# mLSTM state update: a zero-padded 128-column stationary for the 64-row part of each state product

## The chip, the cores and the metric

The kernel runs on one core of one Trainium2 chip. The metric is the device time of one execution in microseconds (us). Engines: PE is TensorE (PEld its weight loads), DVE VectorE, ACT ScalarE, POOL GpSimd, SP the engine that issues the transfers.

## What is computed

The reference is an encoder trunk of two layers on 1024 tokens of width 1024. Each layer normalises its input, projects it once, runs three groups of heads on the projection (mLSTM, HGRN2 and differential attention), gates their outputs and projects them back. The change lies in the mLSTM group: 4 heads of dimension 192, each run forwards and backwards over the sequence. The part of it that matters is the state of a chunk step:

```python
# mlstm_chunkwise, step(carry, inp): ws is exp(dec_s - m_new)
num = einsum("bhts,bhsd->bhtd", w, vb) + g_inter * einsum("bhtd,bhde->bhte", qb, C)
C_new = a * C + einsum("bhs,bhsd,bhse->bhde", ws, kb, vb)   # 192 x 192
n_new = a * n + einsum("bhs,bhsd->bhd", ws, kb)
```

## The kernel before, in words

The program is written in plain order, layer by layer; a scheduler of the tile framework then sets the order of each engine's instructions from its own estimate of their times, so work of different groups is interleaved. Everything is float32; the large projections split each operand into two float32r parts and run three products (L295 for outputs by channel, L308 for outputs by token).

The mLSTM recurrence (L573 to L657) loops over 4 heads (`hd`), over 8 chunks of 128 tokens (`i`) and over two directions (`d`). For each head it loads `xac` (two channel tiles, L581), `xct` (tokens by channels, L583), `vt` (values and a column of ones, 193 columns, L586) and the rows for `W` (L605), makes `q` (L592) and the masked weights `W` (L601 to L611). Then, for each of 16 steps:

- the output product `num` in one bank of PSUM: L627 (`W` by `vt`) into columns 0 to 192, L631 and L632 (`q` by the state `C`, in two tiles of 128 rows) into columns 256 to 448; ACT and DVE combine them and add the result to `hsum` (L633 to L656);
- for the first 7 steps of each direction the state product: GpSimd writes `ks`, the 128 x 192 keys scaled by the weights of their tokens (L639); PE multiplies them with `vt` in two parts, since 192 rows don't fit into one product: 128 key columns (L642) into `C[:, 0]` and 64 key columns (L643) into half of `C[:, 1]`; DVE adds both to the decayed state (L645, L646).

So there are 2 x 4 x 2 x 7 = 112 state products of two matmuls each. Which half of `C[:, 1]` is used depends on the head (`r0` is 0 for even heads, 64 for odd ones); the other half is zeroed once (L618). `ks` has two buffers for both directions together.

PE's order puts these steps between the matmuls of the HGRN2 heads: `hiz`, `hq`, `hff`, `hfb` (projections, 128 stationary columns), the transposes and products L790 to L836, and products with narrow stationaries: L712 and L736 (64 columns; the tiles `lv` hold levels of the HGRN2 scores), L753 and L755 (64 or 32 columns). For a projection block, SP loads four quarters `wraw` (L135), ACT rounds them to `whi` (L136) and GpSimd makes the rest `wlo` (L137); the blocks are numbered (`wlo10` is the `hiz` block of HGRN2 head 2, `wlo13` that of head 3, both in layer 0). SP issues all transfers, one after another, so a transfer that waits for its buffer holds up those behind it.

Of the kernel before, what the change touches and what calls it, by code (L numbers as in the profile page):

```python
# [9 lines left out]
F32 = mybir.dt.float32  # L10
# [4 lines left out]
ALU = mybir.AluOpType  # L15
AX = mybir.AxisListType

P = 128
# [7 lines left out]
MD = 192  # L26
# [64 lines left out]
def trunk(ctx, tc, x_in, positions, w_in, w_out, pvec, rvec, out, dbg=None):  # L91
    nc = tc.nc
# [254 lines left out]
    for l in range(DEPTH):  # L347
# [6 lines left out]
        mu_d = dr.tile([8, S], F32, name=f"mu_{l}")  # L354
        mpl_d = dr.tile([16, 8], F32, name=f"mpl_{l}")

        # ------------------------------------------------------------ input norm
        h = []
        if l:
            npool = ExitStack()  # L360
# [1 line left out]
        for half in range(2):  # L362
# [21 lines left out]
            for k in range(8):  # L384
                ps = ps_mx(f"hT{l}{half}{k}")
                for t4 in range(4):
# [3 lines left out]
                                               op0=ALU.mult, op1=ALU.subtract)  # L390
# [1 line left out]
        npool.close()  # L392
        hpool = ExitStack()
        gp = hpool.enter_context(tc.tile_pool(name=f"hg{l}", bufs=1))
        # ------------------------------------------------------------ mLSTM: conv, q/k/v, gates
        mpool = ExitStack()
        m1 = mpool.enter_context(tc.tile_pool(name=f"mg{l}", bufs=1))
        G = []
# [2 lines left out]
        with tc.tile_pool(name=f"ma{l}", bufs=2) as ma:  # L401
# [38 lines left out]
            for i in range(3):  # L440
                parts = load_win(l, ("xm", i)) if l or i else xm0
                for jj in range(2):
# [9 lines left out]
                    for k in (0, 1, 3, 4):  # L452
                        d = k - 2
# [114 lines left out]
                nc.scalar.activation(t, t, AF.Exp)  # L568
            nc.scalar.activation(flr, flr, AF.Exp, scale=-1.0)

        # ------------------------------------------------------------ mLSTM: chunk recurrence
        with tc.tile_pool(name=f"mc{l}", bufs=1) as mp:
            for hd in range(MH):  # L573
                pr_, hh_ = divmod(hd, 2)
                jA, jC = 3 * pr_ + 2 * hh_, 3 * pr_ + 1
                cA, cC = (slice(0, P), slice(P, MD)) if hh_ == 0 else (slice(64, MD), slice(0, 64))
                r0 = 64 * hh_
                ch = slice(hd * MD, (hd + 1) * MD)
                xac = mp.tile([P, 2, S], F32, tag="m8", name=f"xac{l}{hd}", bufs=2)
                for i, j in enumerate((jA, jC)):  # L580
                    nc.sync.dma_start(xac[:, i], xc_d[j])  # L581
                xct = mp.tile([P, NT, MD], F32, tag="xct", name=f"xcth{l}{hd}")
                nc.sync.dma_start(xct, xct_d.rearrange("(t p) c -> p t c", p=P)[:, :, ch])  # L583
                vt = mp.tile([P, NT, MD + 1], F32, tag="vt", name=f"vth{l}{hd}")
                nc.gpsimd.memset(vt[:, :, MD:], 1.0)
                nc.sync.dma_start(vt[:, :, :MD], v_d.rearrange("(t p) c -> p t c", p=P)[:, :, ch])  # L586
                q = mp.tile([P, 2, S], F32, tag="m8", name=f"q{l}{hd}", bufs=2)
                for i, g in enumerate((G[jA], G[jC][:, hh_])):
                    for half in range(2):
                        sl = slice(half * 512, (half + 1) * 512)  # L590
                        ps = ps_mx(f"q{l}{hd}{i}{half}")
                        nc.tensor.matmul(ps, g, xac[:, i, sl], start=True, stop=True)  # L592
                        nc.scalar.activation(q[:, i, sl], ps, AF.Copy)
                W = {}
                for half in range(2):
                    ps = ps_mx(f"qk{l}{hd}{half}")
                    for c4 in range(4):
                        c = half * 4 + c4
                        sl = slice(c * P, (c + 1) * P)
                        for i in range(2):  # L600
                            nc.tensor.matmul(ps[:, c4 * P:(c4 + 1) * P], xac[:, i, sl], q[:, i, sl], start=(i == 0), stop=(i == 1))  # L601
                    for d in range(2):
                        w = mp.tile([P, 4, P], F32, name=f"W{l}{hd}{half}{d}", tag="W", bufs=4)
                        wf = w.rearrange("p c t -> p (c t)")
                        nc.sync.dma_start(wf, mu_d[d * 4 + hd, half * 512:(half + 1) * 512].partition_broadcast(P))  # L605
                        for c4 in range(4):
                            nc.scalar.activation(w[:, c4], w[:, c4], AF.Exp, scale=-1.0, bias=a_tok[:, d, half * 4 + c4, hd:hd + 1])
                        sg = 1 if d == 0 else -1
                        nc.gpsimd.affine_select(w, w, pattern=[[0, 4], [sg, P]], compare_op=ALU.is_ge, fill=0.0,
                                                base=0, channel_multiplier=-sg)  # L610
                        nc.vector.tensor_tensor(wf, wf, ps, op=ALU.mult)  # L611
                        for c4 in range(4):
                            W[(d, half * 4 + c4)] = w[:, c4]
                hsum = mp.tile([P, NT, MD], F32, tag="m8", name=f"hsum{l}{hd}", bufs=2)
                Cs = []
                for d in range(2):
                    C = mp.tile([P, 2, MD + 1], F32, name=f"C{l}{hd}{d}", tag="C", bufs=2)
                    nc.gpsimd.memset(C, 0.0)  # L618
                    Cs.append(C)
                seen = set()  # L620
                for i in range(NT):
                    for d in range(2):
                        c = i if d == 0 else NT - 1 - i
                        C = Cs[d]
                        sl = slice(c * P, (c + 1) * P)
                        pn = ps_mx(f"num{l}{hd}{d}{c}")
                        nc.tensor.matmul(pn[:, :MD + 1], W[(d, c)], vt[:, c], start=True, stop=True)  # L627
                        n = mp.tile([P, MD + 1], F32, name=f"n{l}{hd}{d}{c}", tag="n", bufs=2)
                        if i > 0:
                            pi = pn[:, 256:256 + MD + 1]  # L630
                            nc.tensor.matmul(pi, q[:, 0, sl], C[:, 0], start=True, stop=False)  # L631
                            nc.tensor.matmul(pi, q[:, 1, sl], C[:, 1], start=False, stop=True)  # L632
                            nc.scalar.activation(n, pi, AF.Copy, scale=ginter[:, d, c, hd:hd + 1])  # L633
                            nc.vector.tensor_tensor(n, pn[:, :MD + 1], n, op=ALU.add)
                        else:
                            nc.scalar.activation(n, pn[:, :MD + 1], AF.Copy)
                        if i < NT - 1:
                            ks = mp.tile([P, MD], F32, name=f"ks{l}{hd}{d}{c}", tag="ks", bufs=2)
                            nc.gpsimd.tensor_scalar(ks, xct[:, c], wsv[:, d, c, hd:hd + 1], None, op0=ALU.mult)  # L639
                            pc = ps_mx(f"st{l}{hd}{d}{c}")  # L640
                            pc2 = pc[r0:r0 + 64, 256:256 + MD + 1]
                            nc.tensor.matmul(pc[:, :MD + 1], ks[:, cA], vt[:, c], start=True, stop=True)  # L642
                            nc.tensor.matmul(pc2, ks[:, cC], vt[:, c], start=True, stop=True)  # L643
                            dc = dec[:, d, c, hd:hd + 1]
                            nc.vector.scalar_tensor_tensor(C[:, 0], C[:, 0], dc, pc[:, :MD + 1], op0=ALU.mult, op1=ALU.add)  # L645
                            nc.vector.scalar_tensor_tensor(C[r0:r0 + 64, 1], C[r0:r0 + 64, 1], dc[r0:r0 + 64], pc2,  # L646
                                                           op0=ALU.mult, op1=ALU.add)
                        den = mp.tile([P, 1], F32, name=f"den{l}{hd}{d}{c}", tag="den", bufs=4)
                        nc.vector.scalar_tensor_tensor(den, n[:, MD:], -1.0, n[:, MD:], op0=ALU.mult, op1=ALU.max)
                        nc.vector.tensor_tensor(den, den, flr[:, d, c, hd:hd + 1], op=ALU.max)  # L650
                        nc.vector.reciprocal(den, den)
                        if c not in seen:
                            seen.add(c)
                            nc.vector.tensor_scalar_mul(hsum[:, c], n[:, :MD], den)
                        else:
                            nc.vector.scalar_tensor_tensor(hsum[:, c], n[:, :MD], den, hsum[:, c], op0=ALU.mult, op1=ALU.add)  # L656
                nc.sync.dma_start(hs_d[hd], hsum)  # L657
        mpool.close()

        # ------------------------------------------------------------ HGRN2  # L660
        def slab(name, tag, bufs=None):
            return gp.tile([P, S], F32, tag=tag, name=f"{name}{l}", bufs=bufs or 1)

# [174 lines left out]
            nc.scalar.activation(yo, ps, AF.Copy, scale=hgs[:, l, hd:hd + 1])  # L838
            nc.sync.dma_start(yT[6 + hd], yo)

        # ------------------------------------------------------------ mLSTM: output gates
        md = hpool.enter_context(tc.tile_pool(name=f"md{l}", bufs=1))

        mo = {}
# [51 lines left out]
            {"i": hgrn_iz, "r": hgrn_rest, "o": mlstm_om, "z": mlstm_zm}[step[0]](int(step[1]))  # L896
        hpool.close()

        # ------------------------------------------------------------ attention
        with tc.tile_pool(name=f"at{l}", bufs=2) as ap, tc.tile_pool(name=f"aw{l}", bufs=1) as aw:  # L900
            def o_post(hd, gt, ss, r):
                rstd(ss, r, P)
# [125 lines left out]
                pend = (hd, gt, ss, r)  # L1028
            o_post(*pend)

        # ------------------------------------------------------------ output projection
        xs = []
        for half in range(2):
            xt = big_tile([P, 4, D], F32, f"xo{l}{half}")
# [122 lines left out]
```

## Time and profile before

| | |
|---|---|
| runs | 2908.21, 2910.12, 2915.83 us, median 2910.12 |
| profiled execution, span from first to last instruction | 2911.1 us (its time beyond the span isn't given) |
| granted TensorE clock, mean | 0.991 |
| PE / DVE / ACT / POOL busy | 97 / 63 / 37 / 22% |

The profile lists one execution. A group names the line, the engine, the operation and the tiles (out<-in), the shape and the number of instructions. A float32 matmul stands as two weight loads and two passes, so 112 matmuls give x224. A matmul counts as busy until a modelled end, and successive matmuls overlap; how long one really takes shows in the distance between two starts.

### The profile page before, as it was taken

The page shows a single profiled execution, that of the slowest core. Times are in us where ns is not written, and L with a number is a line of the kernel's source. Part 1 is how long each engine was busy: PE and PEld are TensorE (multiplying, and loading weights), DVE is VectorE, ACT ScalarE, POOL GpSimd, SP SyncE. Part 2 cuts the span into 40 slices and gives each one's busy share as a digit, 9 for nine tenths or more (in the row PEclk, how much of TensorE's full clock was granted, in tenths as well). Part 3 has the DMA queues.
Part 4 walks back from the last instruction along what each step waited for, and adds up shares of the span by engine and source line. Part 5 has one row for each costly group of instructions (what it writes and reads, how often), then busy time and mean ns, then how long its engine had stood idle before and what let it go on. Part 6 is the DMA issues. An engine that isn't in the chain of part 4 may idle for free. (4 is left out here: it accounts for less than half of the span.)

```text
span 2911.1 us, 49951 instructions
## 1 busy us (share of the span) xinstructions
PE 2821.4 (97%) x20004; PEld 2467.5 (85%) x20004; DVE 1847.9 (63%) x4054; ACT 1070.5 (37%) x2422; POOL 637.3 (22%) x522
## 2 busy tenths in 40 slices
PE   6999999999999999999989999999899999999998
PEld 5888888788888999988879788888898989998886
DVE  6666766575464566696565576666564545767865
ACT  4333323323333445442233423232233324545423
POOL 2122322222123111012211223242121231111112
PEclk9999999999999999999999999999999999999999
DMA  3422212211132001223324211220111221113132
GB/s 119 134 67 67 91 48 73 84 55 45 37 102 95 30 30 37 81 80 93 118 73 131 89 62 52 67 94 30 62 44 44 95 95 30 37 30 109 56 98 104
DMA packets 129864, 210.20 MB, mean 72 GB/s; under 512 B 10832, under 2 KB 60496, under 8 KB 129632
## 3 DMA queue, kind: packets, MB, share of 16 engines
q1 hardware_dynamic: 129632, 207.01, 21.9%
q8 instruction: 157, 2.57, 0.4%
q14 instruction: 75, 0.61, 0.1%
HBM read 156.58 MB, written 50.40 MB: 71 GB/s over the span
## 5 line engine op out<-in xcount | busy, mean ns | idle before, releaser
L137 POOL TENSOR_TENSOR wlo<-wraw,whi 128x512 fp32r<-128x512 f32 x320 | 445.4, 1413 | 1578.5 <-ACT whi L136 1533.6
L1058 PE MATMUL op<-whi,yb 128*128 128x512 f32 x1024 | 333.2, 398 | 0.4 <-DVE xo L1062 0.3
L136 ACT ACTIVATE whi<-wraw 128x512 fp32r<-128x512 f32 x320 | 184.4, 625 | 292.3 <-PE op L1058 85.4
L1062 DVE TENSOR_TENSOR xo<-op,xo 128x512 f32<-128x512 f32 x256 | 174.4, 687 | 96.7 <-PE op L1058 96.6
L308 PE MATMUL pt_hiz<-whi,hh 128*128 128x256 f32 x768 | 225.4, 293 | 6.4 <-DVE hg L674 4.2
L1058 PEld LDWEIGHTS op<-whi,yb 128*128 128x128 f32 x1024 | 192.9, 188 | 45.0 <-DVE xo L1062 1.7
L308 PE MATMUL pt_hiz<-whi,hl 128*128 128x256 f32 x768 | 223.5, 291 | 0.0
L308 PE MATMUL pt_hiz<-wlo,hh 128*128 128x256 f32 x768 | 222.5, 290 | 0.0
L1058 PE MATMUL op<-wlo,yb 128*128 128x512 f32 x512 | 201.9, 394 | 0.0
L639 POOL TENSOR_SCALAR ks<-xcth,wsv 128x192 f32<-128x192 f32 x112 | 111.0, 992 | 388.7 <-PE st L643 345.5
L998 ACT ACTIVATE e<-S,mx 128x1024 f32<-128x1024 f32 x128 | 142.2, 1113 | 142.6 <-DVE mx L995 77.4
L994 DVE TENSOR_REDUCE mx<-S 128x1 f32<-128x1024 f32 x128 | 154.9, 1218 | 36.2 <-PE S L992 35.5
L308 PEld LDWEIGHTS pt_hiz<-whi,hh 128*128 128x128 f32 x768 | 146.4, 191 | 15.1 <-DVE hg L674 5.0
L308 PE MATMUL pt_avz<-whi,hh 128*128 128x256 f32 x512 | 147.8, 289 | 4.4 <-DVE ag L953 4.4
L308 PEld LDWEIGHTS pt_hiz<-wlo,hh 128*128 128x128 f32 x768 | 146.6, 191 | 5.0 <-issue 3.5
L308 PEld LDWEIGHTS pt_hiz<-whi,hl 128*128 128x128 f32 x768 | 146.3, 191 | 3.7 <-issue 2.6
L308 PE MATMUL pt_aqk<-whi,hh 128*128 128x256 f32 x512 | 146.2, 286 | 0.0
L308 PE MATMUL pt_avz<-whi,hl 128*128 128x256 f32 x512 | 145.9, 285 | 0.0
L308 PE MATMUL pt_aqk<-wlo,hh 128*128 128x256 f32 x512 | 145.9, 285 | 0.0
L308 PE MATMUL pt_avz<-wlo,hh 128*128 128x256 f32 x512 | 145.5, 284 | 0.0
L308 PE MATMUL pt_aqk<-whi,hl 128*128 128x256 f32 x512 | 145.2, 284 | 0.0
L1019 PE MATMUL po<-av,wT 128*128 128x128 f32 x1024 | 134.5, 275 | 3.6 <-DVE mx L995 3.4
(358 smaller groups left out, 7560.2 us busy)
## 6 DMA issues: line engine op xcount, KB each, us to landing
wraw<-w_in SPq DMA_DIRECT2D x256, 256.0 KB, 2.8
wraw<-w_out SPq DMA_DIRECT2D x64, 256.0 KB, 2.8
yr<-yT SPq DMA_DIRECT2D x64, 256.0 KB, 2.9
xac<-xcd SPq DMA_DIRECT2D x16, 512.0 KB, 7.2
W<-mu SPq DMA_DIRECT2D x32, 256.0 KB, 3.6
xcd<-xc SPq DMA_DIRECT2D x12, 512.0 KB, 3.0
xct<-tka SPq DMA_DIRECT2D x12, 512.0 KB, 3.4
vd<-tkv SPq DMA_DIRECT2D x12, 512.0 KB, 3.2
```

The costliest lines, as they stand in the source:

```text
L136: nc.scalar.activation(hi[:, o:o + m], rw[:, :m], AF.Copy)
L137: nc.gpsimd.tensor_sub(lo[:, o:o + m], rw[:, :m], hi[:, o:o + m].bitcast(F32))
L308: nc.tensor.matmul(ps[:, :n], a[:, k, ts], b, start=(i == 0), stop=(i == 23))
L639: nc.gpsimd.tensor_scalar(ks, xct[:, c], wsv[:, d, c, hd:hd + 1], None, op0=ALU.mult)
L994: nc.vector.tensor_reduce(mx, ps, axis=AX.X, op=ALU.max)
L998: nc.scalar.activation(e, ps, AF.Exp, scale=QK ** -0.5, bias=mx, accum_out=ls_)
L1019: nc.tensor.matmul(po[:, :P], wT[:, t * P:(t + 1) * P], v[:, t], start=(t == 0), stop=(t == NT - 1))
L1058: nc.tensor.matmul(ps, a[:, j, ts], b[:, cs_], start=(i == 0), stop=(i == 5))
L1062: nc.vector.tensor_tensor(xv, ps, xv, op=ALU.add)
```

## The change

The `ks` tiles become 256 columns wide: 192 hold the keys (from column `k0`, 0 for even heads and 64 for odd ones), 64 hold zeros. The second part of the product takes 128 of these columns, 64 of them zeros, and writes 128 rows of PSUM; DVE reads the same 64 rows as before. So that the zeros have to be written once per head only, four `ks` tiles are made at the head's start (two per direction, each with its memset of 64 columns on GpSimd) and used in turn. To make room, the scratch space for software-made transfers is set to 4096 bytes. The comment lines that became empty are left out here.

```diff
-                cA, cC = (slice(0, P), slice(P, MD)) if hh_ == 0 else (slice(64, MD), slice(0, 64))
+                k0 = 64 * hh_
+                cA, cC = (slice(0, P), slice(P, 256)) if hh_ == 0 else (slice(P, 256), slice(0, P))
...
                 Cs = []
+                kst = []
                 for d in range(2):
+                    for i in range(2):
+                        kt_ = mp.tile([P, 256], F32, name=f"ks{l}{hd}{d}{i}", tag="ks", bufs=4)
+                        nc.gpsimd.memset(kt_[:, MD:] if hh_ == 0 else kt_[:, :64], 0.0)
+                        kst.append(kt_)
                     C = mp.tile([P, 2, MD + 1], F32, name=f"C{l}{hd}{d}", tag="C", bufs=2)
...
-                            ks = mp.tile([P, MD], F32, name=f"ks{l}{hd}{d}{c}", tag="ks", bufs=2)
-                            nc.gpsimd.tensor_scalar(ks, xct[:, c], wsv[:, d, c, hd:hd + 1], None, op0=ALU.mult)
+                            ks = kst[2 * d + i % 2]
+                            nc.gpsimd.tensor_scalar(ks[:, k0:k0 + MD], xct[:, c], wsv[:, d, c, hd:hd + 1], None, op0=ALU.mult)
                             pc = ps_mx(f"st{l}{hd}{d}{c}")
                             pc2 = pc[r0:r0 + 64, 256:256 + MD + 1]
                             nc.tensor.matmul(pc[:, :MD + 1], ks[:, cA], vt[:, c], start=True, stop=True)
-                            nc.tensor.matmul(pc2, ks[:, cC], vt[:, c], start=True, stop=True)
+                            nc.tensor.matmul(pc[:, 256:256 + MD + 1], ks[:, cC], vt[:, c], start=True, stop=True)
...
-    nc = _bacc.Bacc("TRN2", target_bir_lowering=False, num_devices=1)
+    nc = _bacc.Bacc("TRN2", target_bir_lowering=False, num_devices=1, dynamic_dma_scratch_size=4096)
```

In the changed file L627, L631, L632, L642 and L643 are L633, L637, L638, L648 and L649. The scheduler also writes another order, on PE from the second head of layer 0 on. Heads 2 and 3 of layer 0 begin a little earlier among the HGRN2 matmuls; in layer 1 few rows move.

**PE, end of the state steps of head 0 in layer 0**: the step of direction 0, chunk 6, and the projection behind it. Names end in a number of the tile; `st0006` is layer 0, head 0, direction 0, chunk 6. Before:

```order
L627 MATMUL num0006_1836<-vth00_1543,W0010_1593 128x193
L631 MATMUL num0006_1836<-C000_1610,q00_1546 128x193
L632 MATMUL num0006_1836<-C000_1610,q00_1546 128x193
L642 MATMUL st0006_1845<-vth00_1543,ks0006_1843 128x193
L643 MATMUL st0006_1845<-vth00_1543,ks0006_1843 64x193
L308 MATMUL pt_hiz02_0_4523<-whi10_4506,hh00_185 128x256
L308 MATMUL pt_hiz02_0_4523<-wlo10_4505,hh00_185 128x256
```

Now:

```order
L633 MATMUL num0006_1832<-vth00_1543,W0010_1593 128x193
L637 MATMUL num0006_1832<-C000_1614,q00_1546 128x193
L638 MATMUL num0006_1832<-C000_1614,q00_1546 128x193
L648 MATMUL st0006_1840<-vth00_1543,ks0000_1610 128x193
L649 MATMUL st0006_1840<-vth00_1543,ks0000_1610 128x193
L308 MATMUL pt_hiz02_0_4499<-whi10_4482,hh00_185 128x256
L308 MATMUL pt_hiz02_0_4499<-wlo10_4481,hh00_185 128x256
```

The rows stand in the same order; the second state product has 128 rows of output instead of 64. All 112 do.

**GpSimd, from head 0 to head 1 of layer 0**: the multiplications that write `ks`, and the quarters of the projection blocks `wlo10` and `wlo11`. Before:

```order
L639 TENSOR_SCALAR ks0006_1843<-xcth00_1541,wsv_1323 128x192 [waits PE_49,Pool_49]
L137 TENSOR_TENSOR wlo10_4505<-wraw10_1536_4519,whi10_4506 128x512 [waits DMAHW2_49,Activation_49]
L639 TENSOR_SCALAR ks0011_1862<-xcth00_1541,wsv_1323 128x192 [waits PE_49,Pool_49]
L137 TENSOR_TENSOR wlo11_4750<-wraw11_0_4752,whi11_4751 128x512 [waits DMAHW3_49,PE_49,Activation_49]
L137 TENSOR_TENSOR wlo11_4750<-wraw11_512_4756,whi11_4751 128x512 [waits DMAHW4_49,Activation_49]
L137 TENSOR_TENSOR wlo11_4750<-wraw11_1024_4760,whi11_4751 128x512 [waits DMAHW5_49,Activation_49]
L639 TENSOR_SCALAR ks0100_1979<-xcth01_1902,wsv_1323 128x192 [waits DMAHW6_49,PE_49,Pool_49]
```

Now (`ks0000` and `ks0010` are the reused tiles of head 0, `ks0100` is the first of head 1):

```order
L645 TENSOR_SCALAR ks0000_1610<-xcth00_1541,wsv_1323 128x192 [waits PE_49,Pool_49]
L645 TENSOR_SCALAR ks0010_1616<-xcth00_1541,wsv_1323 128x192 [waits PE_49,Pool_49]
L137 TENSOR_TENSOR wlo10_4481<-wraw10_0_4483,whi10_4482 128x512 [waits PE_49,Activation_49]
L137 TENSOR_TENSOR wlo10_4481<-wraw10_512_4487,whi10_4482 128x512 [waits DMAHW5_49,Activation_49]
L137 TENSOR_TENSOR wlo10_4481<-wraw10_1024_4491,whi10_4482 128x512 [waits DMAHW6_49,Activation_49]
L621 MEMSET ks0100_1965 128x64 [waits PE_49,Pool_49]
L645 TENSOR_SCALAR ks0100_1965<-xcth01_1896,wsv_1323 128x192 [waits DMAHW1_49]
L137 TENSOR_TENSOR wlo10_4481<-wraw10_1536_4495,whi10_4482 128x512 [waits DMAHW3_49,Activation_49]
```

The last quarter of `wlo10` stood behind a multiplication of head 0; now it stands behind the memset and the first multiplication of head 1. The memset takes the buffer of `ks0000`, whose last reader is the step shown above.

**SP, from head 1 to head 2 of layer 0**: transfers of the projection blocks 13 and 14 (`wraw`), and of head 2 of the recurrence. Before:

```order
L583 DMA xcth02_2263<-xct_0_177 128x8x192 [waits DMAHW5_49,Pool_49]
L839 DMA yT_0_7_154<-hyo10_4500 128x1024 [waits DMAHW6_49,Activation_49]
L135 DMA wraw13_1536_5277<-w_in 128x512 [waits DMAHW7_49,Pool_49]
L135 DMA wraw14_0_5510<-w_in 128x512 [waits DMAHW1_49,DMAHW0_49,Pool_49]
L135 DMA wraw14_512_5514<-w_in 128x512 [waits DMAHW2_49,Pool_49]
L135 DMA wraw14_1024_5518<-w_in 128x512 [waits DMAHW7_49,Pool_49]
L605 DMA W0210_2315<-mu_0_183 128x512 [waits DMAHW3_49,PE_49]
L586 DMA vth02_2265<-vd_0_178 128x8x192 [waits DMAHW4_49,PE_49]
L605 DMA W0211_2323<-mu_0_183 128x512 [waits DMAHW5_49]
L581 DMA xac02_2260<-xcd_0_3_174 128x1024 [waits DMAHW6_49,PE_49]
L581 DMA xac02_2260<-xcd_0_4_175 128x1024
```

Now:

```order
L584 DMA xcth02_2251<-xct_0_177 128x8x192 [waits DMAHW5_49,Pool_49]
L606 DMA W0210_2303<-mu_0_183 128x512 [waits DMAHW6_49,PE_49]
L845 DMA yT_0_7_154<-hyo10_4476 128x1024 [waits DMAHW7_49,Activation_49]
L587 DMA vth02_2253<-vd_0_178 128x8x192 [waits DMAHW0_49,PE_49]
L606 DMA W0211_2311<-mu_0_183 128x512 [waits DMAHW1_49]
L582 DMA xac02_2248<-xcd_0_3_174 128x1024 [waits DMAHW2_49,PE_49]
L582 DMA xac02_2248<-xcd_0_4_175 128x1024 [waits DMAHW3_49]
L135 DMA wraw13_1536_5253<-w_in 128x512 [waits DMAHW4_49,Pool_49]
L135 DMA wraw14_0_5486<-w_in 128x512 [waits DMAHW5_49,Pool_49]
L663 DMA hsd_0_1_180<-hsum01_1964 128x1536 [waits DMAHW6_49,DVE_49]
```

The last quarter of `wraw13` and the first of `wraw14` stood ahead of `W0210`, `vth02` and `xac02`; now they stand behind them.

## Rows read from the trace of the kernel before

**Rows 1.** The page's header and its table of engines: busy us, share of the span, number of instructions.

```profile
span 2911.1 us, 49951 instructions
...
PE 2821.4 (97%) x20004; PEld 2467.5 (85%) x20004; DVE 1847.9 (63%) x4054; ACT 1070.5 (37%) x2422; POOL 637.3 (22%) x522
```

**Rows 2.** Busy time by stretch (us from the span's start), for two stretches in which a head of the recurrence runs: length, then for PE, PEld, DVE, ACT and POOL busy us and instructions, granted clock, DMA share, GB/s.

```profile
250.00:340.00 90.00, 88.10 (x645) 73.79 (x644) 61.85 (x170) 33.99 (x88) 32.19 (x32) 1.00 0.24 73
340.00:440.00 100.00, 100.00 (x753) 82.22 (x752) 65.82 (x177) 30.29 (x79) 22.54 (x26) 1.00 0.15 51
```

**Rows 3.** What PE waited for, longest first, from 240 to 660 us (layer 0, first row) and from 1650 to 2050 us (layer 1, first row): us in total, times, longest.

```profile
PE q L592 <- DMA xac<-xcd: 3.0, 1, 3.0
...
PE q L592 <- DMA xac<-xcd: 3.3, 2, 2.8
```

**Rows 4.** The instructions of one line (min/median/max ns, first and last start, form): L643 with the idle time of its engine before it, and the weight loads of L632.

```profile
L643 PEld LDWEIGHTS st<-vth,ks x224: 132/134/137, 263.1 to 2032.3; 128*64 128x64 f32 x112
...
  issue: 25.4, 112
...
L632 PEld LDWEIGHTS num<-C,q x224: 189/191/193, 266.8 to 2038.1; 128*128 128x128 f32 x112
```

**Rows 5.** PE's matmuls in order of time (start us, us, line, count of passes): a state product followed by two L295, and later an output product followed by two L295; of the two the second is shown.

```profile
431.38 0.49 PE L642 MATMUL st<-vth,ks 128*128 128x193 f32 x2
431.80 0.54 PE L643 MATMUL st<-vth,ks 128*64 128x193 f32 x2
...
432.60 0.40 PE L295 MATMUL pc_hfb<-hh,whi 128*128 128x512 f32 x1
...
438.70 0.49 PE L627 MATMUL num<-vth,W 128*128 128x193 f32 x2
439.03 0.49 PE L631 MATMUL num<-C,q 128*128 128x193 f32 x2
439.35 0.49 PE L632 MATMUL num<-C,q 128*128 128x193 f32 x2
...
439.91 0.39 PE L295 MATMUL pc_hfb<-hh,wlo 128*128 128x512 f32 x1
```

**Rows 6.** The same view: the start of a state product and the second L308 behind it; the start of L631 and the second and third L308 behind L632.

```profile
467.33 0.49 PE L642 MATMUL st<-vth,ks 128*128 128x193 f32 x2
...
468.45 0.28 PE L308 MATMUL pt_hiz<-whi,hl 128*128 128x256 f32 x1
...
472.74 0.49 PE L631 MATMUL num<-C,q 128*128 128x193 f32 x2
...
473.51 0.29 PE L308 MATMUL pt_hiz<-whi,hl 128*128 128x256 f32 x1
473.63 0.28 PE L308 MATMUL pt_hiz<-whi,hh 128*128 128x256 f32 x1
```

**Rows 7.** The same view: a state product among the 64-column matmuls of L736, and L736 behind an output product.

```profile
476.02 0.60 PE L642 MATMUL st<-vth,ks 128*128 128x193 f32 x2
476.54 0.38 PE L643 MATMUL st<-vth,ks 128*64 128x193 f32 x1
476.55 0.39 PE L736 MATMUL lv<-qp,kt 128*64 128x64 f32 x3
...
476.77 0.89 PE L736 MATMUL lv<-qp,kt 128*64 128x64 f32 x17
477.59 0.59 PE L627 MATMUL num<-vth,W 128*128 128x193 f32 x2
...
600.89 0.49 PE L632 MATMUL num<-C,q 128*128 128x193 f32 x2
601.31 0.72 PE L736 MATMUL lv<-qp,kt 128*64 128x64 f32 x16
601.96 0.39 PE L308 MATMUL pt_hiz<-wlo,hh 128*128 128x256 f32 x1
```

**Rows 8.** Groups of instructions (line, engine, operation, tiles, form, count | busy us, mean ns of one | idle before, releaser).

```profile
L136 ACT ACTIVATE whi<-wraw 128x512 fp32r<-128x512 f32 x320 | 184.4, 625 | 292.3 <-PE op L1058 85.4
...
L618 POOL MEMSET C<- 128x386 f32 x16 | 6.6, 424 | 15.8 <-PE num L632 15.8
...
L585 POOL MEMSET vth<- 128x8 f32 x8 | 0.9, 112 | 29.5 <-DVE hg L674 24.6 <-DMA mpl<-mpl 3.4 <-PE num L627 0.9
```

**Rows 9.** What GpSimd waited for in the whole span: us in total, times, longest.

```profile
POOL ks L639 <- PE st L643: 345.5, 83, 18.5
```

**Rows 10.** GpSimd in order of time around the end of head 0 in layer 0.

```profile
310.46 1.29 POOL L137 TENSOR_TENSOR wlo<-wraw,whi 128x512 fp32r<-128x512 f32 x1
315.55 0.77 POOL L639 TENSOR_SCALAR ks<-xcth,wsv 128x192 f32<-128x192 f32 x1 [3.79 <-PE st L643]
...
324.69 1.99 POOL L639 TENSOR_SCALAR ks<-xcth,wsv 128x192 f32<-128x192 f32 x1
326.64 1.97 POOL L137 TENSOR_TENSOR wlo<-wraw,whi 128x512 fp32r<-128x512 f32 x1
```

**Rows 11.** SP's issues in order of time at the end of head 1 in layer 0, whose last L632 stands in rows 5: the transfers for head 2.

```profile
439.22 0.38 SPq L586 DMA_DIRECT2D vth<-vd  x1
...
440.31 0.85 SPq L581 DMA_DIRECT2D xac<-xcd  x2
```

**Rows 12.** Transfers by line: queue and operation, count, KB each, median us from issue to landing.

```profile
xac<-xcd SPq DMA_DIRECT2D x16, 512.0 KB, 7.2
```

## The prediction, made before the changed kernel was run

> **What bounds the kernel now.** I read the page's header first: TensorE's matmuls are busy 97% of a span of 2911.1 us, VectorE 63%, GpSimd 22% [rows 1]. That is an average, so I cut out stretches in which the mLSTM chunk recurrence runs: there PE is busy 88.1 us of 90 and 100.0 of 100 while DVE is busy 61.9 and 65.8 [rows 2]. Then I asked what PE waits for where the recurrence stands in layer 0 and layer 1: the longest entries are 3.0 and 3.3 us, and nothing there waits for weights [rows 3]. So PE is the bound, and a busy PE is not a PE that computes: a matmul counts as busy from its start to its modelled end. The starts tell more than the busy share, and the rest is read from them.
>
> The state product is a pair, L642 (128 stationary columns) and L643 (64). Its two lines have the same moving tile of 193 columns, and each instruction appears as two weight loads and two passes, hence x224 for 112 pairs. In front of L643's first weight load the loader sits idle in all 112 pairs, 25.4 us together or 0.23 us each, put down to "issue": no semaphore, DMA or engine is named [rows 4]. L627, L631 and L632, which are 128 wide, follow each other without such a gap [rows 5].
>
> **The term that is removed.** I price a whole pair by start times, up to the second matmul of what follows, since the first one after the pair is late as well.
> - Followed by the f32r projection L295: L642 starts at 431.38, the second L295 at 432.60, 1.22 us. The same shape without a narrow stationary, L631 then L632 then L295, goes from 439.03 to 439.91, 0.88 us [rows 5]. Difference 0.34 us.
> - Followed by L308: 467.33 to 468.45, 1.12 us, against 472.74 to 473.51 from the start of L631, 0.77 us [rows 6]. Difference 0.35; I take 0.34 for both.
>
> The first of it stands ahead of L643, which starts 0.42 us after L642 where L632 starts 0.32 after L631; the rest behind it, 0.80 us from L643's start to the second L295 where L632 has 0.56. That is a pause at each change of the number of active columns, in both directions. After the change L643 has the form of L632, so the pair should take the time of L631/L632. The order of PE gives the count: in the kernel before, 88 of 112 pairs are followed by a 128-column matmul and 24 by narrow ones (16 by L736's levels of 64 columns, 8 by L753 and L755). 88 x 0.34 = **29.9 us saved**.
>
> **The 24 others.** Here a change of width was due anyway. L642 starts at 476.02, L643's two passes stand among L736's, the first of which start 0.01 us behind L643, and L627 starts at 477.59: 1.57 us with 20 passes of L736 [rows 7]. Afterwards the width changes one instruction later: L642 0.43 (0.52 now, less 0.09 of the change of width), then L632 to L736 0.42, and 16 passes of L736 take 0.65 [rows 7], so 20 some 0.8: 1.65 us. That is a **loss of about 0.08 us a pair, 24 x 0.08 = 1.9 us**.
>
> **What it adds.** Each of 224 weight loads takes 188 ns instead of 134 [rows 4]. If all of that were exposed, it would be 224 x 0.054 = 12.1 us; at the other end it is nothing. I take nothing, since L632 has loads of 191 ns, and two of them with their passes fit into the 0.32 us from L631 to L632 [rows 4, 5]: beside 193 moving columns a load is hidden. The moving side stays as it is. One rule speaks against the change here: the Trainium skill, "TensorE: Matmul & The Clock Gate", LDWEIGHTS (loading the stationary operand), makes the load's time proportional to the stationary columns, 53 ns more by its figures, an estimate of 12 us over 224 loads if PE paid them. The trace agrees on the size, 54 ns, but not that PE pays it; by the rule alone the sum would be 15 us, by the rows it is 27.
>
> On GpSimd there are 32 memsets of 64 columns. The nearest rows are 0.42 us for 386 columns and 0.11 us for 8 [rows 8], so some 0.16 us each, 5 us on an engine that is 22% busy. The four ks buffers instead of two let the multiplications run ahead; what they wait for L643, 345.5 us in all [rows 9], is not on PE's path. VectorE reads the same 64 rows of the product, each update some 0.25 us earlier. The smaller DMA scratch costs nothing: the transfers are issued by SP, not from GpSimd's software queue [rows 11].
>
> **What it moves.** The scheduler writes another order. Changes of width in PE's order, groups of narrow levels: 118 instead of 114 begin with 64 columns, 39 instead of 42 with fewer; one more net, 0.34 us lost. Two places could make PE wait:
> - GpSimd, head 0 to head 1 of layer 0: the last quarter of wlo10 now stands behind a memset of ks0100, which must wait for L642/L643 of step 6, and behind that head's first multiplication. PE's order reaches the quarter 19 matmuls of L308 after that pair, 19 x 0.12 = 2.3 us [rows 6]. In that time GpSimd has a memset (0.16), a multiplication and the quarter to do: 0.77 and 1.29 us in the quiet case, together 2.2, and 1.99 and 1.97 at worst, together 4.1 [rows 10]. So 0 to 1.8 us; I take 0.5.
> - SP, head 1 to head 2: the last quarter of wraw13 now stands behind the loads of W0210, vth02 and xac02, which wait for the end of head 1. PE has 48 L295, 18 L308 and four q products in between: 48 x 0.23 + 18 x 0.12 = 13.2 us without the q products. In the trace the two xac transfers are issued by 1.8 us after head 1's last L632 starts [rows 5, 11]; add one more issue (0.4), a landing like xac's (7.2 [rows 12]), ScalarE 0.63 [rows 8] and GpSimd 1.29 to 1.97: 11.3 to 12.0 us. Covered; I take 0, with 5 us as the bad end, should the landing take 13 us with all of head 2's data ahead.
>
> Sum: 29.9 - 1.9 - 0.3 - 0.5 = 27.2 us. The 2911.1 us are the profiled execution's span, 1 us above the median 2910.1 of the runs; what lies around the span isn't given. 2910.1 - 27.2 = **2883 us**. The bounds of the terms: 2880 without any loss behind the 29.9, some 2876 if PE's present waits in these stretches shrink by 4 us as well; 2889 with both places at their bad ends; 2895 with the load exposed.
>
> **Rivals.**
> - *Given back to waits.* PE gains some 13 us a layer inside stretches of 400 us, and VectorE's share goes from 68 to about 70%. The two places above reach their bad ends, or the narrow levels wait for VectorE more often. For: q already waits for xac [rows 3], with the same loads ahead. Against: the waits in these stretches are short today. It would return 8 to 16 us: 2891 to 2899.
> - *The load shows.* The pauses go, but the wider loads are exposed, since two of them now come in a row from tiles that GpSimd has only just written: 27 - 12 = 15 us saved, 2895. For: a load of 188 ns is longer than a pass's 0.16 us. Against: L627, L631 and L632 are six such loads in a row, with freshly written C among them, at 0.33 us a product [rows 5]. (This is what the Trainium skill's rule in "TensorE: Matmul & The Clock Gate" would come to.)
> - *Nothing.* The 0.34 us exist, but another engine sets the pace of the recurrence and PE waits elsewhere for as long: 2905 to 2912. Against: PE was busy 100 us of 100.
> - *Slower.* The pause isn't one of width but of the pair itself, such as two products written to the two halves of one bank from the tile GpSimd has just made. It stays, and the longer loads come on top behind it, since nothing runs then that could hide them: 2911 + 12 = 2923. It decides if the gap L642 to L643 stays at 0.42. For: nothing in the trace separates it pair by pair, since every L643 is narrow. Against: L627 and L631 share a bank in the same way and follow each other in 0.33 [rows 5], and L632 to L736, another change of width, has the same 0.42 [rows 7].
> - That the change doesn't do what it says: PE's order shows all 112 second products with 128 columns, so I give it no chance of its own.
>
> **How the numbers follow.** The forecast (2874 to 2890) gets 0.72, given back 0.10, the exposed load 0.05, nothing 0.08, slower 0.05. A measurement of this kernel tells 0.3%, 8.7 us, from no change; faster begins below 2901. So faster 0.87, same 0.08, slower 0.05. The range leaves out nothing and slower, and takes in the others: 2872 to 2900.
>
> **What would show it.** L643's weight loads have 128 columns, 188 ns, and no idle time before them; L642 to L643 takes 0.33 us, L643 to its follower no more than L632 to the same one; pairs before L736 keep one pause, now behind L643. The stretches of the recurrence shorten by some 13 us in each layer and the rest of the program keeps its times. A gap that stays at 0.42 us, a pair that grows towards 0.38, or PE waiting for wlo or wraw around head 1 or head 2 of layer 0 would prove the step wrong to which it belongs.

## The result and the profile after

The changed kernel takes 2886.22 us (2885.62 to 2888.38), the kernel before, on the same chip, 2911.94 (2908.21 to 2915.83). The ratio is 0.9912, with a 95% interval of 0.9897 to 0.9926. The lines of the change stand 6 further down in the new code: the state product is L648 and L649, the output product L633, L637 and L638, the gate levels L718, L742, L759 and L761.

The page's header and engines, to be held against [rows 1]:

```profile
span 2884.8 us, 49995 instructions
...
PE 2795.3 (97%) x20004; PEld 2487.5 (86%) x20004; DVE 1850.4 (64%) x4054; ACT 1071.7 (37%) x2422; POOL 636.0 (22%) x554
```

The span is 26.3 us shorter, and PE's busy time 26.1. The loader (PEld) is busy 20 us more, GpSimd does 32 instructions more: these are what the change adds, and they are not in the time.

The second product (line's instructions, as in [rows 4], then who waited for it: us, times):

```profile
L649 PEld LDWEIGHTS st<-vth,ks x224: 187/190/332, 262.8 to 2003.2; 128*128 128x128 f32 x112
L649 PE MATMUL st<-vth,ks x224: 325/327/371, 263.0 to 2003.4; 128*128 128x193 f32 x112
its engine sat idle before it (us, times) until:
who waited for it (us, times):
  POOL ks L645: 273.0, 69
  POOL ks L621: 64.6, 19
```

The load is 56 ns longer, and the list of idle time before it is empty where 25.4 us in 112 pieces stood.

PE's matmuls in order of time, as in [rows 6] (start us, us, line, passes): a pair that L308 follows.

```profile
471.89 0.49 PE L648 MATMUL st<-vth,ks 128*128 128x193 f32 x2
472.22 0.49 PE L649 MATMUL st<-vth,ks 128*128 128x193 f32 x2
...
472.67 0.28 PE L308 MATMUL pt_hiz<-whi,hl 128*128 128x256 f32 x1
```

L648 to L649 is 0.33 us, and from the pair's start to the second L308 there are 0.78 us, against 1.12 before and 0.77 behind L631 [rows 6]. The same view for a pair among the 64-column levels, as in [rows 7]:

```profile
475.50 0.57 PE L742 MATMUL lv<-qp,kt 128*64 128x64 f32 x12
475.99 0.59 PE L648 MATMUL st<-vth,ks 128*128 128x193 f32 x2
476.43 0.49 PE L649 MATMUL st<-vth,ks 128*128 128x193 f32 x2
476.85 0.45 PE L742 MATMUL lv<-qp,kt 128*64 128x64 f32 x6
```

A step of 0.42 us now stands behind the second product, where the change to 64 columns comes now. The 0.44 ahead of it belongs to the change from the L742 group to L648.

### The profile page after: what moved, and what is told of

It reads as the page before. It is cut to its first block, busy times and chain, and to the rows that moved or that the text cites. A ratio compares the mean times of both kernels' runs of the same rounds, so it can differ in the third digit from the quotient of the medians.

```text
span 2884.8 us, 49995 instructions
## 1 busy us (share of the span) xinstructions
PE 2795.3 (97%) x20004; PEld 2487.5 (86%) x20004; DVE 1850.4 (64%) x4054; ACT 1071.7 (37%) x2422; POOL 636.0 (22%) x554
## 5 line engine op out<-in xcount | busy, mean ns | idle before, releaser
L308 PE MATMUL pt_hiz<-whi,hh 128*128 128x256 f32 x768 | 225.6, 294 | 2.5 <-DVE hg L680 2.5
L308 PE MATMUL pt_hiz<-whi,hl 128*128 128x256 f32 x768 | 224.6, 292 | 0.0
L308 PE MATMUL pt_hiz<-wlo,hh 128*128 128x256 f32 x768 | 223.1, 290 | 0.0
L645 POOL TENSOR_SCALAR ks<-xcth,wsv 128x192 f32<-128x192 f32 x112 | 108.2, 967 | 291.2 <-PE st L649 273.0
L308 PEld LDWEIGHTS pt_hiz<-whi,hh 128*128 128x128 f32 x768 | 146.7, 191 | 7.1 <-DVE hg L680 3.5
L308 PE MATMUL pt_avz<-whi,hh 128*128 128x256 f32 x512 | 147.9, 289 | 4.4 <-DVE ag L959 4.4
L308 PEld LDWEIGHTS pt_hiz<-whi,hl 128*128 128x128 f32 x768 | 146.6, 191 | 2.3 <-issue 1.0
L308 PEld LDWEIGHTS pt_hiz<-wlo,hh 128*128 128x128 f32 x768 | 146.7, 191 | 1.7 <-POOL wlo L137 0.2
L308 PE MATMUL pt_aqk<-whi,hh 128*128 128x256 f32 x512 | 146.1, 285 | 0.0
L308 PE MATMUL pt_avz<-whi,hl 128*128 128x256 f32 x512 | 146.0, 285 | 0.0
L308 PE MATMUL pt_aqk<-wlo,hh 128*128 128x256 f32 x512 | 145.9, 285 | 0.0
L308 PE MATMUL pt_avz<-wlo,hh 128*128 128x256 f32 x512 | 145.6, 284 | 0.0
L308 PE MATMUL pt_aqk<-whi,hl 128*128 128x256 f32 x512 | 145.3, 284 | 0.0
```

The lines of the kernel that those rows point to most:

```text
L308: nc.tensor.matmul(ps[:, :n], a[:, k, ts], b, start=(i == 0), stop=(i == 23))
L645: nc.gpsimd.tensor_scalar(ks[:, k0:k0 + MD], xct[:, c], wsv[:, d, c, hd:hd + 1], None, op0=ALU.mult)
```

## The experiments

Three theories were open after this. **Theory 1**: the pause comes wherever PE's order changes the number of active columns, and the change took out such places. **Theory 2**: the gain comes from what came along, four ks tiles cleared once, a smaller DMA scratch and the scheduler's new order of instructions. **Theory 3**: every narrow product pays by itself, whatever stands beside it. All ratios are to the kernel before on the same chip.

### Everything but the width

The second product takes its 64 columns again; tiles, memsets and scratch stay as changed.

```
+ cN = slice(P, MD) if hh_ == 0 else slice(64, P)
- nc.tensor.matmul(pc[:, 256:256 + MD + 1], ks[:, cC], vt[:, c], ...)
+ nc.tensor.matmul(pc2, ks[:, cN], vt[:, c], ...)
```

> All of the change but the width: four ks tiles of 256 columns, their memsets and the smaller scratch stay, the second product takes 64 columns again. PE's order has as many changes of width as the kernel before (492 instead of 315). Theory 1, a pause at each change of width (0.34 us per pair of changes): the gain goes, 2911 us within 4, the weight load of L649 has 0.23 us of idle time before it again, some 25 us in all. Theory 2, the deeper ks buffers gave the gain: 2886 us.

Measured: 2915.74 us, ratio 1.0005 (0.9996 to 1.0014). The second product's rows:

```profile
L650 PEld LDWEIGHTS st<-vth,ks x224: 132/134/136, 263.2 to 2033.9; 128*64 128x64 f32 x112
...
  issue: 25.4, 112
```

The multiplications that write `ks` wait less for the pair than in the kernel before (288.0 against 345.5 us [rows 9]), but their memsets wait 60.5 us more, and the time is that of before. The loader's idle time is back to the tenth of a microsecond. So tiles, memsets and scratch give nothing. The scheduler's new order is not tested here: with 64 columns the scheduler writes the old one, and all 20004 passes of PE stand in this trace in the order of the kernel before.

Head 0 of layer 0 separates width and order. Up to its end PE's order is the same in both kernels, and the first pair starts at 262.67 us before and at 262.66 now. This is the last of its 14 pairs, with the second L308 behind it, first before, then now:

```profile
326.33 0.49 PE L642 MATMUL st<-vth,ks 128*128 128x193 f32 x2
...
327.44 0.28 PE L308 MATMUL pt_hiz<-whi,hl 128*128 128x256 f32 x1
```

```profile
323.25 0.49 PE L648 MATMUL st<-vth,ks 128*128 128x193 f32 x2
...
324.02 0.28 PE L308 MATMUL pt_hiz<-whi,hl 128*128 128x256 f32 x1
```

The changed kernel is 3.42 us ahead, without any new order. It gains some 0.34 us at each pair; of the 14 x 0.34 = 4.8 us part went to waits that grew, such as one for ScalarE in front of an L295 at 287.46 (1.40 us, 0.91 before).

### The width alone

128 columns, with one ks tile for each direction as before, cleared once; beside the width only that memset, the smaller scratch and the scheduler's new order are left of the change.

```
- for i in range(2): kt_ = mp.tile([P, 256], F32, ..., tag="ks", bufs=4) ...
+ kt_ = mp.tile([P, 256], F32, ..., tag="ks", bufs=2) ...
- ks = kst[2 * d + i % 2]
+ ks = kst[d]
```

> The width alone: 128 columns, but one ks tile per direction instead of two, as deep as before the change. Theory 1: 2886 us within 4, the same gaps as in the changed kernel. Theory 2, the deeper buffers gave the gain: 2905 us or more, with PE waiting for GpSimd's ks.

Measured: 2886.75 us, ratio 0.9909 (0.9894 to 0.9924). The width, with the order that comes with it, is the whole gain: PE's passes stand in the order of the changed kernel. The multiplications' waits for the pair are then 319.6 us in 82 pieces, and cost nothing. With this, with head 0 and with the pairs' starts (below), theory 2 falls, but no run has the new order without the width.

### 96 columns in half of the heads

In heads 0 and 2 the second product takes 96 columns, which is neither the 64 of before nor the 128 beside it.

```
+ if hh_ == 0:
+     nc.tensor.matmul(pc[:96, 256:256 + MD + 1], ks[:, P:P + 96], vt[:, c], ...)
+ else: ... (128 columns)
```

> In the even heads the second product takes 96 columns (64 keys, 32 zeros), in the odd heads 128. Theory 1 as I put it, any change of the number of active columns: the 56 pairs of the even heads pause as they did with 64, so about half of the gain goes, 2898 to 2901 us, and L649's load has 0.23 us of idle time 56 times. Theory 1b, the pause belongs to a column tile of 64 or less, and 96 columns still count as a whole array: 2886 us and no idle time.

Measured: 2887.86 us, ratio 0.9912 (0.9897 to 0.9927). The rows of the 96-column product:

```profile
L650 PEld LDWEIGHTS st<-vth,ks x112: 161/163/163, 262.5 to 1910.6; 128*96 128x96 f32 x112
L650 PE MATMUL st<-vth,ks x112: 325/327/327, 262.7 to 1910.7; 128*96 128x193 f32 x112
its engine sat idle before it (us, times) until:
who waited for it (us, times):
```

The load is that of 96 columns, 163 ns, and nothing idle stands before it. So theory 1 is wrong as I had put it: not every change of the number of columns pauses. What is left is **theory 1b**: the pause comes between products of more than 64 columns and products of 64 or fewer. (Where between 65 and 96 the border lies was not tried.)

### All three products narrow

The kernel before, with its first product cut into two halves of 64 columns: more narrow products, but none among wide ones inside the pair.

```
- nc.tensor.matmul(pc[:, :MD + 1], ks[:, cA], vt[:, c], ...)
+ for u in range(2):
+     nc.tensor.matmul(pc[64*u:64*u + 64, :MD + 1], ks[:, cA.start + 64*u:cA.start + 64*u + 64], vt[:, c], ...)
```

> The kernel before with the first product split into two of 64 columns each, so that a step has three narrow products and still one change in and one out. Theory 1: the pauses stay as they were; the extra product costs at most 112 x 0.33 = 37 us if it takes its own time, nothing if the halves run side by side: 2911 to 2948 us. Theory 3, each narrow product costs 0.34 us by itself: two more per step, 112 x 2 x 0.34 = 76 us on top, 2985 us or more.

Measured: 2901.85 us, ratio 0.9963 (0.9949 to 0.9977), below all that was expected. PE's order of time shows what was missed (L643 is the two halves, L644 the former L643):

```profile
306.94 0.49 PE L632 MATMUL num<-C,q 128*128 128x193 f32 x2
307.36 0.55 PE L643 MATMUL st<-vth,ks 128*64 128x193 f32 x4
307.74 0.49 PE L644 MATMUL st<-vth,ks 128*64 128x193 f32 x2
308.16 0.50 PE L295 MATMUL pc_hfb<-hh,wlo 128*128 128x512 f32 x1
```

The four passes of the two halves take 0.38 us, where two passes of one product take 0.33: halves in different columns run side by side. So the third product is nearly free, the steps of 0.42 stand at the two ends of the group (L632 to L643, L644 to L295), and L643 to L644 has none. That is against theory 3: narrow behind narrow pays nothing. In PE's order this kernel has 451 changes of width against 492 before; 20 pairs of changes less at 0.34 us are 7 of some 12 us. PE's waits for other engines are also 6.0 us shorter (73.6 against 79.6 us in the whole program); what shortened them is open.

### The price by itself: one more product in each pair

Between L648 and the second product stands one with 16 moving columns, into columns of pc that nothing reads; once with 128 stationary columns, once with 64.

```
  nc.tensor.matmul(pc[:, :MD + 1], ks[:, cA], vt[:, c], ...)
+ nc.tensor.matmul(pc[:, 460:476], ks[:, cA], vt[:, c, :16], ...)                              # wide
+ nc.tensor.matmul(pc[:64, 460:476], ks[:, cA.start:cA.start + 64], vt[:, c, :16], ...)        # or narrow
```

> The changed kernel with one more product in each of the 112 pairs, between L648 and its second product: 16 moving columns of vt, the first product's own 128 stationary columns, into 16 columns of pc that nothing reads. It is the yardstick for the next run. It costs at least its own weight load, near the 187 ns of the load rows of L649, since 16 moving columns are too few to hide the next load: 112 x 0.19 = 21 us, 112 x 0.22 = 25 us with its own passes. Theory 1b (the pause belongs to 64 or fewer columns): 2907 to 2912 us, no idle time in front of the next load. Rival (the pause belongs to the place, to a product into another part of the same bank): some 112 x 0.34 = 38 us more, 2945 or above.

> As the run before, but the extra product takes 64 of the 128 stationary columns and writes 64 partitions; order, inputs and the place in pc are the same. Theory 1b: a narrow product between two 128-column ones brings a pause, 0.2 to 0.34 us each, less some 0.05 us for the shorter weight load: 17 to 32 us above the run before, 2925 to 2943 us, and the 25 and 112 us of 'issue' idle come back in front of the loads. Rival (the pause belongs to the pair of the kernel before, its second product's input or its half of the bank): no more than the run before, or some 5 us less.

Measured: wide 2907.55 us, ratio 0.9984 (0.9975 to 0.9994); narrow 2931.92, ratio 1.0068 (1.0052 to 1.0084). Both as theory 1b has it. PE's order of time, first of the wide kernel, then of the narrow one:

```profile
300.72 0.49 PE L648 MATMUL st<-vth,ks 128*128 128x193 f32 x2
301.05 0.29 PE L649 MATMUL st<-vth,ks 128*128 128x16 f32 x2
301.19 0.57 PE L650 MATMUL st<-vth,ks 128*128 128x193 f32 x2
```

```profile
304.14 0.49 PE L648 MATMUL st<-vth,ks 128*128 128x193 f32 x2
304.56 0.29 PE L649 MATMUL st<-vth,ks 128*64 128x16 f32 x2
304.78 0.59 PE L650 MATMUL st<-vth,ks 128*128 128x193 f32 x2
```

A product with half the columns, and loads of 134 instead of 190 ns, costs 24.4 us more: 112 x 0.22 us. The narrow one starts 0.42 us behind L648 where the wide one starts 0.33 behind, and its successor 0.22 behind it instead of 0.14. Its line in the narrow kernel:

```profile
L649 PEld LDWEIGHTS st<-vth,ks x224: 132/134/137, 265.0 to 2046.5; 128*64 128x64 f32 x112
...
  issue: 25.4, 112
```

The 25.4 us of idle loader are there again, with another product, another place in the bank and a pair that has none of its own. The rival, that the pause is one of the old pair, falls. (PE's order is not quite the same in the two kernels; the pause is read from the starts.) That 0.22 is less than 0.34 fits the two shorter loads, 2 x 0.056 us, which can show here, since the wide one's step of 0.14 us is shorter than its load of 0.19: 0.22 + 0.11 = 0.33.

### A step further: the narrow groups kept whole

If a change of width costs, then so do the 128-column products that the scheduler puts into the middle of a group of narrow levels, as at 475.99 above. Here these groups are issued with priority, so that nothing comes between; first the levels of L718 and L742, then also those of L759 and L761.

```
+ with tc.high_priority():
      for c in range(NT): ...   # the products of one level
```

> The changed kernel, with the narrow products of the gate levels at L713 and L743 issued as one unbroken group each (high priority), so that no 128-column product lands inside a group. In TensorE's order the changes between 64 or fewer and more columns fall from 315 to 248, some 33 pairs of changes less. Theory 1b, by 0.34 us for a pair of changes: 33 x 0.34 = 11 us faster than the change, 2875 us. Rival (the groups were split because other engines were not ready, so the pause only becomes a wait): 2886 us or more, with waits for DVE in front of those groups.

> As the run before, with the third narrow group (L759 and L761) kept whole as well: 192 changes of width in TensorE's order against 315, 61 pairs less. Theory 1b: 61 x 0.34 = 21 us faster than the change, 2865 us; with narrow products of other column groups partly side by side already, half of that, 2875 us. Rival: 2886 us or more, the pauses come back as waits for DVE and ACT in front of the groups.

Measured: 2861.80 us, ratio 0.9821 (0.9804 to 0.9838), and 2839.41, ratio 0.9749 (0.9735 to 0.9764). Both directions are right and both sizes about twice the forecast; the second is the fastest of all versions, 46.8 us below the change. PE's order of time, a group in it (L744 is the former L742):

```profile
462.12 1.15 PE L744 MATMUL lv<-qp,kt 128*64 128x64 f32 x32
463.20 0.59 PE L648 MATMUL st<-vth,ks 128*128 128x193 f32 x2
```

A whole group of 32 passes takes 1.08 us. In the changed kernel such a group was often cut, here in three:

```profile
482.51 0.91 PE L742 MATMUL lv<-qp,kt 128*64 128x64 f32 x22
483.35 0.59 PE L633 MATMUL num<-vth,W 128*128 128x193 f32 x2
...
484.53 0.45 PE L742 MATMUL lv<-qp,kt 128*64 128x64 f32 x6
484.90 0.59 PE L648 MATMUL st<-vth,ks 128*128 128x193 f32 x2
485.33 0.49 PE L649 MATMUL st<-vth,ks 128*128 128x193 f32 x2
485.75 0.34 PE L742 MATMUL lv<-qp,kt 128*64 128x64 f32 x4
486.02 0.39 PE L308 MATMUL pt_hiz<-whi,hh 128*128 128x256 f32 x1
```

The three parts take 0.84, 0.37 and 0.27 us, together 1.48. To that come the late starts of the wide products between: 0.42 to 0.43 instead of 0.33 at each edge. So the two cuts cost some 0.8 us, 0.4 each, near the 0.34 of the pair. The idle time put down to "issue" goes with the cuts, first in the changed kernel, then in the last one:

```profile
L742 PEld LDWEIGHTS lv<-qp,kt x1920: 132/138/143, 218.6 to 2260.8; 128*64 128x64 f32 x192
...
  issue: 16.6, 54
```

```profile
L744 PEld LDWEIGHTS lv<-qp,kt x1920: 132/138/143, 218.7 to 2213.6; 128*64 128x64 f32 x192
...
  issue: 3.7, 11
```

The trace of the change has 157 unbroken runs of narrow products, that of the last kernel 96.

Then why twice the forecast? By spans the last kernel gains 2884.8 - 2837.5 = 47.3 us, and two parts of it have nothing to do with the price of a pause. PE's waits for other engines, summed over the whole program, fall from 79.6 to 67.1 us, by 12.5. And the changed kernel has 41.0 us of half clock (granted clock 0.50, 1.2 GHz) between start and end, this one 13.7 (the first 100 us and the last stretch left out in both); the difference of 27.3 us at half speed is worth up to 13.6 us. What is left is some 21 us, and theory 1b's 61 x 0.34 is 21. For the first of the two kernels the same sum gives 2884.8 - 2860.8 = 24.0 us, less 8.6 of waits (71.0 are left) and up to 3.4 of half clock (34.1 are left): 12.0, against 11 forecast. So the price held and the surplus came from waits and clock, by this estimate; the two overlap a little. The rival had it the wrong way round, since the waits became shorter; why they did is not shown.

## Why the prediction was right, point by point

- **PE is the bound.** Right: PE's busy time and the span fell by the same 26 us, and PE's waits for other engines are 79.6 us in the whole program before and after. GpSimd's waits for the pair went from 345.5 us to 337.6 (273.0 and 64.6), without a trace in the time.
- **88 pairs at 0.34 us, 29.9 us.** Right in size. By the starts of the pairs the excess over the wide form was 0.34 us before (59 pairs that L295 or L308 follow) and is 0.00 after. The terms that belong to the width give 29.9 - 1.9 - 0.3 = 27.7 us. The kernel with everything but the width has, like the changed one, 41.0 us of half clock, and its span of 2912.9 us against 2884.8 gives 28.1 us for the width and the order that comes with it.
- **24 pairs among narrow levels, 1.9 us lost.** Right in kind: the pause now stands behind the second product, as between 476.43 and 476.85. The size is an estimate: priced by the usual steps of the neighbouring rows, all of them together lose 1 to 2 us, and no run shows it by itself.
- **The wider load, 0 of at most 12.1 us.** Right. The loads take 190 ns (I had written 188, where [rows 4] has 191 for that form), and the pair's two products follow each other in 0.33 us. The Trainium skill's "TensorE: Matmul & The Clock Gate", LDWEIGHTS section, makes the load's time proportional to the columns; the three rows 134, 163 and 190 ns at 64, 96 and 128 columns agree that it grows with them, but twice the columns take only 1.4 times as long, and beside 193 moving columns PE pays for none of it. Beside 16 it does: the extra wide product costs 2907.55 - 2886.22 = 21.3 us, 0.19 each, as long as a load.
- **GpSimd from head 0 to head 1, 0.5 us lost.** Wrong: nothing was lost. GpSimd in order of time there, then PE's pairs of steps 5 and 6 of head 0 (direction 0):

```profile
304.78 2.70 POOL L137 TENSOR_TENSOR wlo<-wraw,whi 128x512 fp32r<-128x512 f32 x2
307.42 0.43 POOL L621 MEMSET ks<- 128x64 f32 x1
...
309.31 1.44 POOL L137 TENSOR_TENSOR wlo<-wraw,whi 128x512 fp32r<-128x512 f32 x1 [0.91 <-ACT whi L136]
```

```profile
305.69 0.49 PE L648 MATMUL st<-vth,ks 128*128 128x193 f32 x2
...
318.28 0.49 PE L648 MATMUL st<-vth,ks 128*128 128x193 f32 x2
```

The memset runs without a wait behind the quarter before it, and the last quarter then waits for ScalarE, not for the memset. I had named the wrong buffer: the memset of `ks0100` doesn't take that of `ks0000`, whose last reader is step 6, but that of `ks0001`, whose last reader is step 5. Step 5 starts at 305.69 us; step 6 starts at 318.28, 11 us behind the memset, which therefore can't have waited for it.
- **SP from head 1 to head 2, 0 us.** Right: between 240 and 660 us PE's matmuls wait nowhere for wlo or wraw, and the loader 0.2 us in all.
- **By stretch.** Some 13 us in each layer were expected. The first score product of attention (`S`) in layer 0 starts 12.5 us earlier than before, that of layer 1 26.4, the end 26.3: 12.5 and 13.9.
- **The mechanism, "a pause at each change of the number of active columns".** Right for 64 against 128, too wide as a rule: 96 columns beside 128 have none. The Trainium skill's "TensorEngine Tiling (Array Packing)", Tiling Modes, lists 128, 64 and 32 columns as configurations and says that changing the mode drains the engine (Key Properties). The traces fit this: 96 columns, for which no mode is listed, behave like 128, and going to 64 columns and back costs 0.34 us here. That the pause is this drain is not shown by any run.

What is left: 25.7 us by the medians and 26.3 by the spans were measured, 27.2 predicted. Of PE's waits, the sum from 240 to 660 us went from 9.4 to 10.4. The changed kernel also has 41.0 us of half clock between start and end where the kernel before has 30.7, up to 5 us of loss. Busy time by stretch (length, PE, PEld, DVE, ACT, POOL busy us and instructions, granted clock, DMA share, GB/s), and PE's order in both, show how the two go together:

```profile
320.00:330.00 10.00, 8.10 (x83) 7.69 (x82) 10.00 (x17) 3.46 (x7) 8.51 (x8) 1.00 0.35 107
330.00:333.40 3.40, 3.40 (x15) 3.40 (x14) 3.30 (x9) 1.41 (x5) 0.86 (x3) 0.50 0.41 91
```

```profile
328.67 0.59 PE L633 MATMUL num<-vth,W 128*128 128x193 f32 x2 [1.90 <-DVE n L640]
...
330.86 0.85 PE L633 MATMUL num<-vth,W 128*128 128x193 f32 x2
331.50 0.85 PE L637 MATMUL num<-C,q 128*128 128x193 f32 x2
```

PE waited 1.90 us for VectorE, and soon behind it the granted clock is 0.50 (1.2 GHz) for 3.4 us, with L633 to L637 in 0.64 us instead of 0.33. Such stretches come and go from version to version. That they make up all of the difference is argued, not shown.

## What to carry to other kernels

Read the starts, not the busy share: an engine that is 97% busy lost some 50 us (28 in the pairs, some 21 in the cut groups) to pauses that no wait names, and the loader's idle time put down to "issue" in front of one form was the trace of it. Price a form against its neighbour in the same program (a narrow product against the wide one with the same moving tile), pad the narrow one where the array would be empty anyway, and then keep the narrow groups that must stay in one piece. When a gain comes out at twice the forecast, take off what waits and clock changed before you raise the price: 47 us looked like a higher price, and 26 of them were waits and clock.

## What the runs showed that I had not expected

- 96 stationary columns cause no pause beside 128; 64 cause 0.34 us in and out.
- Two halves of 64 columns from the same moving tile take 0.38 us together, against 0.33 for one: cutting a 128-column product in two cost almost nothing, and the kernel became some 12 us faster, 7 of them by 20 pairs of changes less where the neighbour was narrow already.
- A wait of 1.9 us on PE was followed by 3.4 us at 1.2 GHz, in the changed kernel from 330.0 us on; the kernel before shows the same at 452.7 us, behind a wait of 1.90 us for L674. At half speed that is some 1.7 us lost besides the wait.
